# Encoder layer on one core: value products of a query-tile pair on aligned key blocks, with one 128-column product for both edge blocks

## The chip, the cores and the metric

The kernel runs on one core of a Trainium2 chip. The metric is the device time of one execution in microseconds (us). Three runs of the kernel before gave 2041.09, 2041.80 and 2042.51 us, median 2041.80.

## The reference

One encoder layer over 1024 tokens of width 1024: a half-step SwiGLU block, a hybrid mixer and a second half-step SwiGLU block, each followed by a layer norm. The change lies in the mixer's attention branch. It has twelve heads of width 128 in three groups of four, with windows and dilations (128,1), (512,4) and (2048,16):

```python
def dilated_window_attention(q, k, v, rel_bias_g, window, dilation):
    half = window // (2 * dilation)      # 64 in all three groups
    ...
    band = jnp.abs(off) <= half
    mask = band[None] & valid[:, None, :]
    logit_add = jnp.where(mask[None], bias[:, None], NEG_INF)
    s = einsum(q, k) * scale + logit_add
    mx = jnp.max(s, axis=-1, keepdims=True)
    p = jnp.exp(s - mx)
    den = jnp.sum(p, axis=-1)
    o = einsum(p, v) / den
```

A group with dilation d is d independent sequences of 1024/d tokens, and a query sees the keys at most 64 places away in its own sequence: group 0 is one sequence of 1024, group 1 four of 256, group 2 sixteen of 64. The weights p are exactly zero wherever the mask holds. The three groups' outputs are then joined by their softmax denominators, projected, gated and merged with a Fourier branch.

## The kernel before

All large matrix products (both SwiGLU blocks, the input projection, the output projection) are block products with seven multiplications for eight, in three float32r terms each. They are the jobs of the program: a fixed list for TensorE. Everything else is a node with a cost, a due time and the buffers it takes and gives back. A planner (`Flow`, L75 to L280) walks the job list at build time with a clock for each engine and writes out the order of each engine's instructions. Small TensorE work of the attention is a floating node (`F`): it is put between two jobs once its inputs are planned to be ready at least 0.8 us earlier. Loads (`Q`) go to SP's DMA queue, stores and a few loads to POOL's. At run time each engine and each queue works strictly in the written order and waits on semaphores.

The planner counts three pools: 8 PSUM banks, 46 pages of 128x1024 floats, and 11 halves of 128x512 floats (`NS2`, tag "s2"). A load that takes a half is put off while fewer than four others would remain free, unless its user is due within 5 us (L185). A load whose half is still being used by an earlier owner waits at the head of SP's queue, and whatever is behind it there waits too.

Attention of a head (`attention`, L1656) runs beside the projection jobs of the next head. It takes the head's query and key pages, its values (one page, `load_values`, L1623, three DMAs from DRAM in groups 0 and 1, rows of 128 floats) and its bias. The 1024 queries are cut into steps. A step is two query tiles of 128 in groups 0 and 1, four in group 2. Each step is one chain: `scores` on TensorE (L1685), `add_bias` and `top` on VectorE (L1699, L1709), `exps` on ScalarE (L1714), `turn` on TensorE (transposes of 128 columns, L1730), `turned` on ScalarE (PSUM to SBUF, L1739), `values` on TensorE (L1755, L1760), `keep` on ScalarE (L1773 to L1778).

Twenty of the forty steps are pairs with windows of 192 keys (`w == 192`, `split_`): the first and last tile of group 0's sequence, and both tiles of each of group 1's four sequences. They go like this before the change. The later tile comes first. The transposes give three blocks of 128 keys by 128 queries: the later tile's keys shifted by 64 with respect to the tiles, the earlier tile's keys shifted likewise, and a mixed block with 64 keys of each tile. `blank` (two VectorE memsets of 64x128, L1747, L1748) clears two quarters of the 256 columns that the mixed block is spread into, and `turned` copies the first two blocks (128x256) and then the mixed block's two halves (64x128 each, L1742, L1743). `values` makes one product of 256 columns of the mixed block's keys with both tiles (L1755) and two products of 128 columns (L1760). In group 0 the pair's order is turned round (`turned_round`, L1703), and `combine` reads group 1's statistics with the odd tiles first (L1996).

The planner also prepares pieces of the output projection's weights during this stage (`keep_halves`, L1932: 28 pieces, each one SP load, one ScalarE pass, one VectorE pass and two POOL stores, in three halves). `SPREAD` (L1887) chooses the jobs by which they are due.

Of the kernel before, what the change touches and what calls it, by code (L numbers as in the profile page):

```python
# [12 lines left out]
AF = mybir.ActivationFunctionType  # L13
# [3 lines left out]
P = 128  # L17
S0 = 1024
# [56 lines left out]
class Flow:  # L75
# [207 lines left out]
class Builder:  # L283
# [10 lines left out]
    def half(self, name, dt=F32):  # L294
        return self.sb.tile([P, 512], dt, name=name, tag="s2", bufs=NS2)
# [12 lines left out]
def kernel(  # L308
# [909 lines left out]
    VJ, v_stored, VW, vb, VT = {}, {}, {}, {}, {}  # L1218
# [48 lines left out]
    for i, (to, x0, x1) in enumerate((("t1", "b11", "b12"), ("t3", "b12", "b22"), ("t2", "t1", "b22"),  # L1267
# [6 lines left out]
        n = Q(J[("a", 1 + i), 4], 1.15, copy, [vtn[x0]] if x0 in vtn else [], lead=0.0)  # L1274
# [348 lines left out]
    def load_values(g, h):  # L1623

        c0 = (g * SLOTS + h) * P

        def rows(dst, row0, p_step, n, n_step):
            ap = [[p_step * QW, dst.shape[0]], [n_step * QW, n], [1, P]]
            nc.sync.dma_start(dst, bass.AP(tensor=v_d.tensor, offset=v_d.offset + row0 * QW + c0, ap=ap))
        t = page(f"v{g}{h}")  # L1630
        tv = as_k(t)
        vf = {}
        if g == 0:
            rows(tv[:, 0:7], 64, 1, 7, P)
            rows(tv[0:64, 7:8], S0 - 64, 1, 1, 1)
            rows(tv[64:128, 7:8], 0, 1, 1, 1)
            for i in range(7):
                vf[64 + P * i, P] = tv[:, i, :]
            vf["edge", 0] = tv[:, 7, :]
        elif g == 1:  # L1640
            rows(tv[:, 0:4], 4 * 64, 4, 4, 1)
            rows(tv[0:64, 4:8], 4 * 192, 4, 4, 1)
            rows(tv[64:128, 4:8], 0, 4, 4, 1)
            for i in range(4):
                vf[256 * i + 64, P] = tv[:, i, :]
                vf["edge", 256 * i] = tv[:, 4 + i, :]
# [9 lines left out]
    def attention(idx, g, h, qk, qk_nodes):  # L1656
        c = PC["q", idx]
        env = {}
        qv = Q(J[c, 4], 0.5, lambda: env.__setitem__("v", load_values(g, h)),
               [(n, 4.0) for m in range(8) for n in (v_stored[g, m] if g == 2 else [v_stored[g, m]])], 12.0, pages=1)  # L1660
        qb = Q(J[c, 4], 0.1, lambda: env.__setitem__("b", load_bias(g, h)),
               [(shear_n[g * SLOTS + h], 4.0)] + ([bias_done[idx - 2]] if idx >= 2 else []), 12.0)
        if g == 0:
            steps = [[(i, P * i - 64, 256) for i in (a, a + 1)] for a in (1, 3, 5)]
            steps.append([(7, S0 - 192, 192), (0, 0, 192)])
        elif g == 1:
            steps = [[(2 * r + 1, 256 * r + 64, 192), (2 * r, 256 * r, 192)] for r in range(4)]
        else:
            steps = [[(i, P * i, P) for i in range(a, a + 4)] for a in (0, 4)]
        col0 = 8 * g  # L1670
# [3 lines left out]
        def one(si, step):  # L1674
# [28 lines left out]
            turned_round = g == 0 and tiles == [0, 7]  # L1703

            def top():
                if h not in stats:
                    stats[h] = kb.small([P, 24, 2], "stat", bufs=2)
                cols = slice(7, None, -7) if turned_round else slice(s0, s0 + stepc * (n - 1) + 1, stepc)
                nc.vector.tensor_reduce(stats[h][:, cols, 0], p3(), AX.X, OP.max, negate=True)  # L1709

            def exps():
                for i in range(n):
                    k = 7 - 7 * i if turned_round else s0 + i * stepc
                    nc.scalar.activation(p3()[:, i, :], p3()[:, i, :], AF.Exp, bias=stats[h][:, k, 0:1], scale=1.0,  # L1714
                                         accum_out=stats[h][:, k, 1:2])
            (qa, ka, _), (qb_, kb_, _) = step[0], step[1]
            if w == 192:

                cuts = [0, 256, 128]
                where = [(qa, ka, P, 0, 0), (qb_, kb_ + 64, P, 0, 1), (qa, ka + P, 64, 0, 2), (qb_, kb_, 64, 64, 2)]  # L1720
# [11 lines left out]
            split_ = w == 192  # L1732

            def turned():
                if not split_:
                    st["t"] = half(f"pT{g}{h}{si}")
                t = st["t"]
                k = 2 * P if split_ else len(cuts) * P
                nc.scalar.activation(t[:, :k], st["tp"][:, :k], AF.Copy)  # L1739
                if split_:  # L1740

                    nc.scalar.activation(t[0:64, 3 * P:], st["tp"][0:64, k:k + P], AF.Copy)  # L1742
                    nc.scalar.activation(t[64:P, k:3 * P], st["tp"][64:P, k:k + P], AF.Copy)  # L1743

            def blank():
                st["t"] = half(f"pT{g}{h}{si}")
                nc.vector.memset(st["t"][0:64, 2 * P:3 * P], 0.0)  # L1747
                nc.vector.memset(st["t"][64:P, 3 * P:], 0.0)  # L1748

            def values():  # L1750
                st["o"] = bk = bank(f"pv{g}{h}{si}")
                seen = set()
                pt = st.pop("t")
                if split_:
                    nc.tensor.matmul(bk[:, :2 * P], env["v"]["edge", kb_], pt[:, 2 * P:], start=True, stop=False,  # L1755
                                     skip_group_check=True)
                for qt, kc, rows, r0, sl in where[:2] if split_ else where:
                    at = tiles.index(qt) * P
                    last = split_ or sum(x[0] == qt for x in where) == 1 + (qt in seen)
                    nc.tensor.matmul(bk[:, at:at + P], env["v"][kc, rows], pt[:, sl * P:(sl + 1) * P],  # L1760
                                     start=not split_ and qt not in seen, stop=last, skip_group_check=True)
                    seen.add(qt)

            def keep():
                if "pv" not in env:
# [214 lines left out]
    def combine(h):  # L1980
# [18 lines left out]

# [559 lines left out]
```

## Time and profile before

| what | value |
|---|---|
| median of three runs | 2041.80 us (2041.09 to 2042.51) |
| the profiled execution's own time | 2041.54 us |
| its span, first to last instruction | 2039.8 us |
| TensorE busy | 2028.7 us |
| VectorE, ScalarE, POOL busy | 1372.8, 907.5, 283.2 us |
| granted TensorE clock | 0.999 |

The span is 1.74 us shorter than the execution's own time. In the trace a float32 product is two matmul records (two passes), a float32r product or a transpose is one; records of neighbouring matmuls overlap, so what a matmul costs is read from the start of one to the start of the next. PE is TensorE's matmuls, PEld its weight loads, SPq and POOLq are DMA issues of the two queues, and a number in square brackets behind a row is the idle time of the engine before it, with what ended it.

### The profile page before, as it was taken

What the parts mean: (1) busy time and instruction counts of PE and PEld (TensorE: products, weight loads), DVE (VectorE), ACT (ScalarE), POOL (GpSimd) and SP (SyncE); (2) the same over time, 40 slices, a digit from 0 to 9 for tenths busy, and PEclk for the clock granted to TensorE, in tenths of its full rate; (3) what the DMA queues carried; (4) which work ended last, traced back from release to release, by engine and by line L of the source; (5) the groups of instructions that cost most, each with busy time, mean ns of one, the idle gap of its engine ahead of it and who ended that gap; (6) DMA issues with size and microseconds to landing.
All of it is one profiled execution on the core that took longest, in us unless ns stands there. A gap on an engine that the chain in (4) does not pass through costs nothing.

```text
span 2039.8 us, 26286 instructions
## 1 busy us (share of the span) xinstructions
PE 2028.7 (99%) x9531; PEld 1700.2 (83%) x9531; DVE 1372.8 (67%) x1988; ACT 907.5 (44%) x1440; POOL 283.2 (14%) x486
## 2 busy tenths in 40 slices
PE   9999999999999999999999999999999999999998
PEld 7888888888888898888888888888888888888886
DVE  7765665576676768665656666887876665575565
ACT  6433333454454224655556444336533333355432
POOL 0133211111001122222122110000011111110000
PEclk9999999999999999999999999999999999999999
DMA  5789998899953366655345669784157887668752
GB/s 206 234 269 284 292 299 260 248 338 369 339 186 130 115 242 212 217 182 153 118 134 169 228 224 348 279 328 170 68 195 232 267 250 215 177 214 288 236 186 94
DMA packets 179251, 458.52 MB, mean 225 GB/s; under 512 B 21362, under 2 KB 55490, under 8 KB 178576
## 3 DMA queue, kind: packets, MB, share of 16 engines
q1 hardware_dynamic: 130864, 299.42, 42.5%
q0 software_dynamic: 48256, 157.41, 25.8%
q8 instruction: 75, 1.23, 0.2%
q14 instruction: 56, 0.46, 0.1%
HBM read 341.69 MB, written 185.29 MB: 258 GB/s over the span
## 4 chain that ended last, share of the span: by engine, by line
PE 98%; DMA 1%; ACT 1%; DVE 0%; issue 0%; SPq 0%; DVEq 0%
PE Ab L496 14%; PE Aa L496 14%; PE Aq L496 8%; PE Db L496 6%; PE Da L496 6%; PE As L496 5%; PE Dq L496 3%; PE Zb L865 3%; PE Xa L865 3%; PE Xb L865 3%; PE Za L865 3%; PE Ds L496 2%; PE wA L2384 2%; PE Va L865 1%; PE Vb L865 1%; PE Yb L865 1%
## 5 line engine op out<-in xcount | busy, mean ns | idle before, releaser
L1714 ACT ACTIVATE p<-p,stat 128x192 f32<-128x192 f32 (+2 forms) x96 | 42.2, 441 | 24.0 <-DVE stat L1709 22.4
L338 POOL DMA_DIRECT2D n_spill<-y x16 | 9.4, 586 | 300.8 <-DVE y L1062 244.4
L338 POOL DMA_DIRECT2D hsba<-t2b x21 | 11.6, 550 | 265.6 <-DVE t2b L731 265.6
L338 POOL DMA_DIRECT2D hsaa<-t2a x21 | 12.4, 589 | 244.8 <-DVE t2a L731 240.0
L1504 DVE SCALAR_TENSOR_TENSOR oq<-Dq,b_cols,t2q 128x512 f32<-128x512 f32 x12 | 11.8, 985 | 50.3 <-PE Dq L496 50.3
L634 ACT ACTIVATE t2b<-Ab 128x512 f32<-128x512 f32 x21 | 12.6, 598 | 63.5 <-PE Ab L496 63.5
L727 DVE TENSOR_TENSOR t2b<-Db,t2b 128x512 f32<-128x512 f32 x21 | 14.5, 691 | 39.1 <-PE Db L496 39.1
L1699 DVE SCALAR_TENSOR_TENSOR p<-sc,bias 128x512 f32<-128x512 f32 (+1 forms) x40 | 24.8, 621 | 20.6 <-PE sc L1685 18.7
L727 DVE TENSOR_TENSOR t2a<-Da,t2a 128x512 f32<-128x512 f32 x21 | 14.5, 690 | 35.3 <-PE Da L496 35.3
L634 ACT ACTIVATE t2a<-Aa 128x512 f32<-128x512 f32 x21 | 12.5, 596 | 55.7 <-PE Aa L496 55.7
L1760 PEld LDWEIGHTS pv<-pT,v 128*128 128x128 f32 x240 | 32.6, 191 | 3.4 <-ACT pT L1739 1.0
L1685 PE MATMUL sc<-oq,oq 128*128 128x192 f32 (+2 forms) x192 | 34.8, 322 | 0.0
L1760 PE MATMUL pv<-pT,v 128*128 128x128 f32 x240 | 33.0, 275 | 0.6 <-ACT pT L1739 0.6
L1685 PEld LDWEIGHTS sc<-oq,oq 128*128 128x128 f32 x192 | 29.4, 190 | 1.7
L719 DVE TENSOR_TENSOR t3b<-Db,t3b 128x512 f32<-128x512 f32 x21 | 14.5, 691 | 22.1 <-PE Db L496 20.0
L496 PE MATMUL Da<-Xs40h,usa 128*128 128x512 f32 x84 | 29.3, 389 | 0.0
L496 PE MATMUL Da<-Xs41h,usa 128*128 128x512 f32 x84 | 29.3, 389 | 0.0
L496 PE MATMUL Db<-Zs40h,usb 128*128 128x512 f32 x84 | 29.3, 389 | 0.0
L496 PE MATMUL Db<-Zs41h,usb 128*128 128x512 f32 x84 | 29.3, 389 | 0.0
L719 DVE TENSOR_TENSOR t3a<-Da,t3a 128x512 f32<-128x512 f32 x21 | 14.5, 690 | 21.6 <-PE Da L496 18.3
L1709 DVE TENSOR_REDUCE stat<-p 128x2 f32<-128x384 f32 (+2 forms) x40 | 24.3, 619 | 1.0
L634 ACT ACTIVATE t3a<-Aa 128x512 f32<-128x512 f32 x21 | 12.5, 596 | 26.9 <-PE Aa L496 26.8
(7647 smaller groups left out, 7428.9 us busy)
## 6 DMA issues: line engine op xcount, KB each, us to landing
qa<-hsas SPq DMA_DIRECT2D x43, 256.0 KB, 6.8
qa<-tdat SPq DMA_DIRECT2D x43, 256.0 KB, 5.4
qb<-hsbs SPq DMA_DIRECT2D x43, 256.0 KB, 4.3
ga<-in_ffn_gu_dram SPq DMA_DIRECT2D x21, 512.0 KB, 8.9
ua<-in_ffn_gu_dram SPq DMA_DIRECT2D x21, 512.0 KB, 10.0
gb<-in_ffn_gu_dram SPq DMA_DIRECT2D x21, 512.0 KB, 4.6
ub<-in_ffn_gu_dram SPq DMA_DIRECT2D x21, 512.0 KB, 5.8
qb<-tdbt SPq DMA_DIRECT2D x33, 256.0 KB, 5.0
```

The lines of the kernel that those rows point to most:

```text
L338: nc.gpsimd.dma_start(*a, **kw)
L496: nc.tensor.matmul(out, pick(w, a)[:, k * P:(k + 1) * P], self.cols(xn, b, k), start=first and k == 0 and ti == 0, stop=last and k == kt - ...
L634: nc.scalar.activation(H[c, t], B[c, "B"], AF.Copy)
L719: nc.vector.tensor_sub(H[c, "t3"], B[c, "D"], H[c, "t3"])
L727: nc.vector.tensor_sub(H[c, "t2"], B.pop((c, "D")), H[c, "t2"])
L865: nc.tensor.matmul(bank_, a, b, start=first and ti == 0, stop=last and ti == len(todo) - 1, skip_group_check=True)
L1685: nc.tensor.matmul(sv[:, i, :], qk[0][:, qt * P:(qt + 1) * P], qk[1][:, k0:k0 + w], start=True, stop=True, skip_group_check=True)
L1699: stt(p3(), sv, scale, bv, op0=OP.mult, op1=OP.add)
L1709: nc.vector.tensor_reduce(stats[h][:, cols, 0], p3(), AX.X, OP.max, negate=True)
L1714: nc.scalar.activation(p3()[:, i, :], p3()[:, i, :], AF.Exp, bias=stats[h][:, k, 0:1], scale=1.0, accum_out=stats[h][:, k, 1:2])
L1760: nc.tensor.matmul(bk[:, at:at + P], env["v"][kc, rows], pt[:, sl * P:(sl + 1) * P], start=not split_ and qt not in seen, stop=last, skip_ ...
L2384: nc.tensor.matmul(B["w", bk, m], X4.cols(xn, a, k)[:, m * P:(m + 1) * P], pick(w, b), start=new and k == 0 and ti == 0, stop=k == 3 and t ...
```

## The change

In a split pair the earlier tile now comes first. Its first 128 columns of weights are its own 128 keys, and columns 64 to 192 of the later tile are the later tile's own 128 keys: key blocks that are aligned with the query tiles. The middle block has 64 keys of the later tile for the earlier tile's queries (in its upper 64 rows) and 64 keys of the earlier tile for the later tile's queries (in its lower 64 rows). By the mask only the second 64 queries of the earlier tile see the former, and only the first 64 queries of the later tile see the latter. Two quarters of the block are therefore zero by the exponential itself. With its two column halves swapped in the copy, the block is one operand of 128 columns for the output columns 64 to 192.

So the memsets go, three ScalarE copies become two, and the product of 256 columns becomes one of 128 which comes last and accumulates over both tiles' columns. The values are loaded in aligned blocks of 128 keys and, for the edges, into a half (`te`): five DMAs in place of three for a head of group 0 (640 KB in place of 512), four in place of three for one of group 1 (768 KB in place of 512). The half is taken with the load and given back after the head's last value product. The view of the bias goes through its 64-column step downwards, the statistics' columns lose their turned order, and the planner's costs of the changed nodes and `SPREAD` (14 to 10, so all 28 pieces of output weights are due four jobs earlier) are set anew.

```diff
+        te = half(f"ve{g}{h}").rearrange("p (k n) -> p k n", k=4) if g < 2 else None
         if g == 0:
             rows(tv[:, 0:7], 64, 1, 7, P)
-            rows(tv[0:64, 7:8], S0 - 64, 1, 1, 1)
-            rows(tv[64:128, 7:8], 0, 1, 1, 1)
+            rows(tv[:, 7:8], 0, 1, 1, 1)
+            rows(te[:, 0:1], S0 - P, 1, 1, 1)
+            rows(te[0:64, 1:2], P, 1, 1, 1)
+            rows(te[64:128, 1:2], S0 - 192, 1, 1, 1)
...
         elif g == 1:
-            rows(tv[:, 0:4], 4 * 64, 4, 4, 1)
-            rows(tv[0:64, 4:8], 4 * 192, 4, 4, 1)
-            rows(tv[64:128, 4:8], 0, 4, 4, 1)
+            for i in range(2):
+                rows(tv[:, 4 * i:4 * i + 4], 4 * P * i, 4, 4, 1)
+                rows(te[64 * i:64 * i + 64], 4 * (P - 64 * i), 4, 4, 1)
...
         qv = Q(J[c, 4], 0.5, lambda: env.__setitem__("v", load_values(g, h)),
-               [...], 12.0, pages=1)
+               [...], 12.0, pages=1, halves=int(g < 2))
...
-            steps.append([(7, S0 - 192, 192), (0, 0, 192)])
+            steps.append([(0, 0, 192), (7, S0 - 192, 192)])
         elif g == 1:
-            steps = [[(2 * r + 1, 256 * r + 64, 192), (2 * r, 256 * r, 192)] for r in range(4)]
+            steps = [[(2 * r, 256 * r, 192), (2 * r + 1, 256 * r + 64, 192)] for r in range(4)]
...
-                    bv = bass.AP(tensor=bias.tensor, offset=bias.offset, ap=[list(bias.ap[0]), [64, 2], [1, 192]])
+                    bv = bass.AP(tensor=bias.tensor, offset=bias.offset + 64, ap=[list(bias.ap[0]), [-64, 2], [1, 192]])
...
                 nc.scalar.activation(t[:, :k], st["tp"][:, :k], AF.Copy)
                 if split_:
-                    nc.scalar.activation(t[0:64, 3 * P:], st["tp"][0:64, k:k + P], AF.Copy)
-                    nc.scalar.activation(t[64:P, k:3 * P], st["tp"][64:P, k:k + P], AF.Copy)
-
-            def blank():
-                st["t"] = half(f"pT{g}{h}{si}")
-                nc.vector.memset(st["t"][0:64, 2 * P:3 * P], 0.0)
-                nc.vector.memset(st["t"][64:P, 3 * P:], 0.0)
+                    to, at = (x[:, k:k + P].rearrange("p (s q) -> p s q", s=2) for x in (t, st["tp"]))
+                    nc.scalar.activation(to, at[:, ::-1, :], AF.Copy)
...
-                if split_:
-                    nc.tensor.matmul(bk[:, :2 * P], env["v"]["edge", kb_], pt[:, 2 * P:], start=True, stop=False,
-                                     skip_group_check=True)
-                for qt, kc, rows, r0, sl in where[:2] if split_ else where:
+                for qt, kc, rows, r0, sl in where:
...
+                if split_:
+                    nc.tensor.matmul(bk[:, 64:192], env["v"]["edge", ka], pt[:, 2 * P:3 * P], start=False, stop=True,
+                                     skip_group_check=True)
...
-            nb = [V(0.35, blank, [n2], slack=8.0, halves=1)] if split_ else []
-            n4 = S(0.95 if split_ else 0.54, turned, [f2] + nb, frees=1, halves=0 if split_ else 1, slack=8.0)
-            f3 = F(0.88 if split_ else 0.22 * len(where), values, [n4], 1, hgives=1, gives=1 if end else 0)
+            n4 = S(0.6 if split_ else 0.54, turned, [f2], frees=1, halves=1, slack=8.0)
+            f3 = F(0.22 * (len(where) + int(split_)), values, [n4], 1, hgives=1 + int(end and g < 2), gives=1 if end else 0)
...
-    SPREAD = lambda k: 2 * k + 14
+    SPREAD = lambda k: 2 * k + 10
...
-                gather(t[32 * j:32 * j + 32, 1], 8 + 4 * (1 - j), 0, [[4 * 48, 32], [48, 4], [1, 8]])
+                gather(t[32 * j:32 * j + 32, 1], 8 + 4 * j, 0, [[4 * 48, 32], [48, 4], [1, 8]])
```

More of the change, by code (lines that the diff above doesn't have):

```diff
@@ L1634, in load_values @@
             rows(tv[:, 0:7], 64, 1, 7, P)
-            rows(tv[0:64, 7:8], S0 - 64, 1, 1, 1)
-            rows(tv[64:128, 7:8], 0, 1, 1, 1)
+            rows(tv[:, 7:8], 0, 1, 1, 1)
+            rows(te[:, 0:1], S0 - P, 1, 1, 1)
+            rows(te[0:64, 1:2], P, 1, 1, 1)
+            rows(te[64:128, 1:2], S0 - 192, 1, 1, 1)
             for i in range(7):
                 vf[64 + P * i, P] = tv[:, i, :]
-            vf["edge", 0] = tv[:, 7, :]
+            vf[0, P] = tv[:, 7, :]
+            vf[S0 - P, P] = te[:, 0, :]
+            vf["edge", 0] = te[:, 1, :]
         elif g == 1:
-            rows(tv[:, 0:4], 4 * 64, 4, 4, 1)
-            rows(tv[0:64, 4:8], 4 * 192, 4, 4, 1)
-            rows(tv[64:128, 4:8], 0, 4, 4, 1)
+            for i in range(2):
+                rows(tv[:, 4 * i:4 * i + 4], 4 * P * i, 4, 4, 1)
+                rows(te[64 * i:64 * i + 64], 4 * (P - 64 * i), 4, 4, 1)
+            for i in range(8):
+                vf[256 * (i % 4) + P * (i // 4), P] = tv[:, i, :]
             for i in range(4):
-                vf[256 * i + 64, P] = tv[:, i, :]
-                vf["edge", 256 * i] = tv[:, 4 + i, :]
+                vf["edge", 256 * i] = te[:, i, :]
         else:
@@ L1659, in attention @@
         qv = Q(J[c, 4], 0.5, lambda: env.__setitem__("v", load_values(g, h)),
-               [(n, 4.0) for m in range(8) for n in (v_stored[g, m] if g == 2 else [v_stored[g, m]])], 12.0, pages=1)
+               [(n, 4.0) for m in range(8) for n in (v_stored[g, m] if g == 2 else [v_stored[g, m]])], 12.0, pages=1,
+               halves=int(g < 2))
         qb = Q(J[c, 4], 0.1, lambda: env.__setitem__("b", load_bias(g, h)),
@@ L1701, in one @@
             s0, stepc = (col0 + tiles[0] // 2, 4) if g == 1 else (col0 + tiles[0], tiles[1] - tiles[0])
-            turned_round = g == 0 and tiles == [0, 7]
             def top():
@@ L1719, in one @@
                 cuts = [0, 256, 128]
-                where = [(qa, ka, P, 0, 0), (qb_, kb_ + 64, P, 0, 1), (qa, ka + P, 64, 0, 2), (qb_, kb_, 64, 64, 2)]
+                where = [(qa, ka, P, 0, 0), (qb_, kb_ + 64, P, 0, 1)]
             else:
@@ L1734, in turned @@
             def turned():
-                if not split_:
-                    st["t"] = half(f"pT{g}{h}{si}")
-                t = st["t"]
+                st["t"] = t = half(f"pT{g}{h}{si}")
                 k = 2 * P if split_ else len(cuts) * P
@@ L1753, in values @@
                 pt = st.pop("t")
+                for qt, kc, rows, r0, sl in where:
+                    at = tiles.index(qt) * P
+                    last = not split_ and sum(x[0] == qt for x in where) == 1 + (qt in seen)
+                    nc.tensor.matmul(bk[:, at:at + P], env["v"][kc, rows], pt[:, sl * P:(sl + 1) * P],
+                                     start=not seen if split_ else qt not in seen, stop=last, skip_group_check=True)
+                    seen.add(qt)
                 if split_:
-                    nc.tensor.matmul(bk[:, :2 * P], env["v"]["edge", kb_], pt[:, 2 * P:], start=True, stop=False,
+                    nc.tensor.matmul(bk[:, 64:192], env["v"]["edge", ka], pt[:, 2 * P:3 * P], start=False, stop=True,
                                      skip_group_check=True)
-                for qt, kc, rows, r0, sl in where[:2] if split_ else where:
[L1758 to L1762, printed above, removed]
             def keep():
```

5 lines of the change are left out of this document (2 added, 3 removed).

## The prediction

> **What bounds the kernel now.** I read the page's busy times and chain first, then who waits for whom on TensorE, then busy time by stage (in each row the stretch, its length, and PE, PEld, DVE, ACT, POOL, granted clock, DMA share, GB/s).
>
> ```profile
> span 2039.8 us, 26286 instructions
> ...
> PE 2028.7 (99%) x9531; PEld 1700.2 (83%) x9531; DVE 1372.8 (67%) x1988; ACT 907.5 (44%) x1440; POOL 283.2 (14%) x486
> ...
> PE 98%; DMA 1%; ACT 1%; DVE 0%; issue 0%; SPq 0%; DVEq 0%
> ```
>
> ```profile
> PE warm L2463 <- DVE eps L334: 1.4, 1, 1.4
> PE Aa L496 <- ACT Xa110h L386: 0.8, 1, 0.8
> PE pv L1760 <- ACT pT L1739: 0.6, 1, 0.6
> PE Aa L496 <- DVE Xa110l L392: 0.2, 1, 0.2
> ```
>
> ```profile
> 784.73:1122.43 337.70, 337.14 (x1734) 288.43 (x1733) 213.81 (x354) 197.28 (x460) 71.37 (x126) 1.00 0.56 173
> 1122.43:1270.00 147.57, 147.57 (x685) 123.38 (x685) 98.06 (x131) 69.36 (x98) 19.67 (x36) 1.00 0.73 262
> 1270.00:1410.00 140.00, 140.00 (x723) 119.37 (x722) 111.80 (x216) 54.24 (x97) 2.17 (x4) 1.00 0.71 267
> 1410.00:2029.00 619.00, 619.00 (x2749) 512.97 (x2748) 410.42 (x536) 251.23 (x340) 59.42 (x101) 1.00 0.64 205
> ```
>
> TensorE makes 98% of the chain, at full granted clock. It idles only in the first microseconds, in the tail after its last matmul, and once in between: 0.56 us in the attention stage (784.73 to 1122.43), before a value product. So a microsecond of product removed there is a microsecond off the time, as long as the work that follows is ready that much earlier; and what VectorE (214 of 338 us) or ScalarE (197) is spared is worth nothing by itself.
>
> **The change part by part.** First the products. The rows give start, duration and count of records. Two split pairs stand next to each other here; a step of four 128-column products follows:
>
> ```profile
> 851.31 0.59 PE L1755 MATMUL pv<-pT,v 128*128 128x256 f32 x2
> 851.74 0.61 PE L1760 MATMUL pv<-pT,v 128*128 128x128 f32 x4
> 852.18 0.60 PE L1755 MATMUL pv<-pT,v 128*128 128x256 f32 x2
> 852.62 0.61 PE L1760 MATMUL pv<-pT,v 128*128 128x128 f32 x4
> ```
>
> ```profile
> 820.48 1.05 PE L1760 MATMUL pv<-pT,v 128*128 128x128 f32 x8
> 821.37 0.60 PE L1730 MATMUL pt<-ident,p 128*128 128x128 f32 x4
> ```
>
> Start to start, the 256-column product takes 0.43 to 0.44 us (851.31 to 851.74), two products of 128 columns take 0.44 (851.74 to 852.18), so 0.22 each; the four take 0.89, again 0.22. A split pair's values cost 0.87 us before and 3 x 0.22 = 0.66 to 0.67 after: 0.20 to 0.21 less. There are 20 such pairs (four heads, one in group 0 and four in group 1); the by-form group counts 40 records of two passes each:
>
> ```profile
> L1755 PE MATMUL pv<-pT,v 128*128 128x256 f32 x40 | 11.9, 378 | 0.0
> ```
>
> That is 20 x 0.21 = 4.2 us (4.0 to 4.4 by the rounding of the rows). The new product comes last and accumulates over the second half of one tile and the first half of the other. No row shows an accumulation across two outputs; bounded by 0.22 (a 128-column product) and 0.44 (the one it replaces), I take 0.22, because today's products accumulate over columns just written at that price. The lower bound cannot be undercut: the columns are streamed. Weight loads stay at three per pair.
>
> The Trainium skill (TensorE: Matmul & The Clock Gate, Back-to-back issue gap) gives 134 cycles for an isolated matmul of 128 columns and 262 for 256, but says that in a real stream of load and matmul the weight load counts too, and that 128 columns then take about 81 ns in place of 56. With four units of the page's gap for a product of float32, an estimate, the isolated figures give 0.22 and 0.44 us, as the rows above do; by the sustained figure a 128-column product would be 0.32 us, and twenty would gain about 2 us in place of 4.2 (this is rival 3). The trace does not agree with the sustained figure.
>
> Next ScalarE and VectorE, one split pair:
>
> ```profile
> 831.54 0.38 ACT L1739 ACTIVATE pT<-pt 128x256 f32<-128x256 f32 x1
> 831.82 0.26 ACT L1742 ACTIVATE pT<-pt 64x128 f32<-64x128 f32 x1
> 832.09 0.27 ACT L1743 ACTIVATE pT<-pt 64x128 f32<-64x128 f32 x1
> ```
>
> ```profile
> 829.07 0.17 DVE L1747 MEMSET pT<- 64x128 f32 x1
> 829.30 0.17 DVE L1748 MEMSET pT<- 64x128 f32 x1
> ```
>
> VectorE loses 40 memsets of 0.17 us, each 0.23 from start to start: 9 us. ScalarE trades two copies of 0.26 and 0.27 for one of 128x128 with its halves swapped, between 0.26 (64x128) and 0.38 (128x256); I take 0.27, nearest to the same column count, so 20 x 0.26 = 5 us less. Both engines have over 120 us free in the stage, so I count zero. The gain cannot be more than the 0.56 us of TensorE's one wait there; if the swapped copy cost the full 0.38, the chain of a pair would still be 0.15 us shorter than now. The bias view that steps backwards and the statistics' new columns keep their instruction count and shapes: between zero and, if the backward step slowed the 384-element pass, the 0.1 us between its 0.55 and the 0.69 of a 512-element one, 20 times, beside TensorE's jobs: zero.
>
> Now the loads. The rows of SP's queue come first; TensorE's first use of the first head's values is the row at 820.48 above, and of the second head's the one at 851.31:
>
> ```profile
> 785.83 3.05 SPq L1629 DMA_DIRECT2D v<-v_spill  x3
> ...
> 807.76 2.15 SPq L1629 DMA_DIRECT2D v<-v_spill  x3
> ```
>
> ```profile
> DMA to landing us min/median/max: 3.2/6.7/10.7
> ```
>
> Four heads get two DMAs more and four one more, 12 issues at about 0.7 us (2.15/3) on SP: 9 us of queue in 338, and 1.5 MB at 173 GB/s, 9 us of transfer at a DMA share of 0.56. Values are issued 35 and 44 us ahead of use and land within 10.7, so even a doubled issue and landing (3 and 11 us) stays hidden: zero. What stands behind them in SP's queue is the next pair's weights, treated under the rivals; POOL's queue gets nothing.
>
> The half `te` is held from the load to the head's last value product: 785.83 to 834.5 and 807.76 to 861.2, about 50 us. Eight heads in 338 us hold 8 x 50 / 338 = 1.2 of the 11 halves on average, two at times. Against this the split step takes its output half only at `turned`, not at `blank` (829.07 to 831.54, 2.5 us, so 20 x 2.5 / 338 = 0.15 halves). The pool gets tighter by about one. This delays nodes that want a half, first the 28 weight pieces, whose users are products of a later stage. `SPREAD` makes these due four jobs earlier, about 4 x 2.75 = 11 us (a job is a row such as the one below) plus the floats between. All of a piece moves: one SP load, one ScalarE and one VectorE pass, two POOL stores. They cross loads of values and pair weights on SP and the bias and spill stores on POOL; TensorE reads none of them in this stage, so zero.
>
> ```profile
> 960.52 2.74 PE Aq L496 x12
> ```
>
> Last, the planner: with other costs it writes another order from here to the end. The later stages have TensorE busy in 147.57 of 147.57 us, 140.00 of 140.00 and 619.00 of 619.00; I count zero, and bound it by a gain of 0.56 (the one wait) and a loss of 2.2, four waits of that size.
>
> The sum: the profiled execution's 2041.54 - 4.2 = 2037.3 us. Its own time is 0.26 below the median of the runs, 2041.8, which is what the new runs will be set against: 2041.8 - 4.2 = 2037.6; with a little of the one wait gone, 2037.5. The 0.2% that a measurement of this kernel can tell from no change is 4.1 us, so the forecast lies on that edge.
>
> **The rivals.**
>
> (1) The saved columns come back as waits. The place is the end of the attention, where the last head's exponentials meet the first gate's sigmoids on ScalarE:
>
> ```profile
> 1105.78 1.28 ACT L1496 ACT_TABLE_LOAD   x1
> 1107.07 0.69 ACT L1496 ACTIVATE os<-As,b_cols 128x512 f32<-128x512 f32 x1
> 1107.78 1.28 ACT L1714 ACT_TABLE_LOAD   x1
> 1109.07 0.40 ACT L1714 ACTIVATE p<-p,stat 128x128 f32<-128x128 f32 x1
> ...
> 1111.11 0.57 ACT L1739 ACTIVATE pT<-pt 128x512 f32<-128x512 f32 x1
> ```
>
> ```profile
> 1111.74 0.49 PE L1760 MATMUL pv<-pT,v 128*128 128x128 f32 x2 [0.56 <-ACT pT L1739]
> ```
>
> Two table loads of 1.28 us lie ahead of the copy that TensorE's only wait is for. The planner does not know them. If the new order puts one more sigmoid between the last steps, two more loads come: 2.6 us on that chain, 2037.5 + 2.6 = 2040.1. If it puts the sigmoid after the last step, the wait goes: 2037.0. For it speaks that this chain has no cover left. Against: it is one place, and the first gate is due when it was. The Trainium skill (ScalarE: Activation LUTs, What ACT_TABLE_LOAD costs) puts a switch at 1283 ns and a further 1380 ns of drain; by it two more switches would be 5.3 us and the time 2042.8, an estimate. The load agrees with the rows; the drain they do not show, since the exponential starts 1.29 us after its load.
>
> (2) Slower: the tighter halves block SP's queue. It happens today that a piece waits at the head of the queue for a half which is still being stored (the row gives total, times and longest wait):
>
> ```profile
> SPq L1941 <- DMA wot_d<-wot10l: 12.2, 1, 12.2
> ```
>
> ```profile
> 880.14 0.33 SPq L570 DMA_DIRECT2D uq<-in_in_pairs_dram  x1
> 880.53 2.30 SPq L1629 DMA_DIRECT2D v<-v_spill  x3
> 883.00 12.16 SPq L1941 DMA_DIRECT2D wot40r<-wtt  x2
> 905.39 0.33 SPq L570 DMA_DIRECT2D gq<-in_in_pairs_dram  x1
> ```
>
> ```profile
> 915.44 0.48 PE L496 MATMUL Aq<-Ys20h,t12q7h 128*128 128x512 f32 x1
> ```
>
> Now a values load can wait there too, with pair weights behind it. The weights issued at 880.14 feed the product at 915.44, 35 us later. Landing, taken at the 10.7 us of the slowest values load, and the sums and splits in between leave some 20 us, an estimate: a block must exceed that before TensorE stops. Two blocks like the longest one here, back to back (24.3 us), stop it for 4.3 and eat the gain: 2041.8. Three (36.5) give 2037.5 + 16.5 = 2054. Against: no stop shows today with blocks of 12, the pieces now finish earlier, and the planner puts off values loads while the pool is short.
>
> (3) The change does not do what it says: the 128-column edge product is held by its weight loads (records of 0.19 us, two passes, 0.38 us) and not by its columns. It would then save 0.43 - 0.38 = 0.05, in all 1 us: 2040.8. Against: the same loads precede today's 128-column products, which follow each other at 0.22.
>
> ```profile
> L1755 PEld LDWEIGHTS pv<-pT,v 128*128 128x128 f32 x40 | 7.1, 189 | 1.2
> ```
>
> **How the numbers follow.** The forecast, 2036.9 to 2038.2 for itself: 0.58, of which 0.35 lies beyond the 0.2% edge (2037.7). The wait gone or more (2036.2 to 2036.9): 0.07, faster. Rival 1's loss, or other small waits from a new order (2038.2 to 2042): 0.19, within 0.2%. Rival 3: 0.03, within. Rival 2, from 2042 up: 0.13, about 0.11 of it slower by more than 0.2% (over 2045.9). So faster 0.42, same 0.47, slower 0.11. The range 2036.2 to 2042.0 takes in both bounds of the unknowns and leaves out rival 2.
>
> **What would show it.** No 256-column record in the value products, three starts 0.22 apart in a split pair, the copies down to two per pair at 0.38 and about 0.27, no memsets, 4.2 us fewer between the first and the last projection job of the attention stage, and TensorE's waits no longer than one 0.6. The prediction is wrong if a wait on ScalarE or a DMA of over 1 us appears among TensorE's waits, if the values' first product waits for its load, or if SP's waits at the values' line pass 20 us.

## The result and the profile after

The changed kernel takes 2036.47 us (median; 2036.13 to 2037.19) beside 2041.64 for the kernel before, a ratio of 0.9975 with a 95% interval of 0.9965 to 0.9984: 5.2 us, 0.25% faster. The profiled execution took 2036.13 us, its span 2034.3.

The page of the changed kernel, busy time and chain:

```profile
span 2034.3 us, 26254 instructions
...
PE 2025.1 (100%) x9531; PEld 1697.1 (83%) x9531; DVE 1366.1 (67%) x1948; ACT 900.2 (44%) x1418; POOL 283.0 (14%) x486
...
PE 99%; DMA 1%; DVE 0%; ACT 0%; issue 0%; SPq 0%; DVEq 0%
```

All waits of TensorE in it:

```profile
PE warm L2460 <- DVE eps L334: 1.4, 1, 1.4
PE Aa L496 <- DVE Xa110l L392: 0.2, 1, 0.2
```

The wait before a value product is gone; what is left lies in the first microseconds. To see where the time went, the two traces are cut at the same TensorE instructions: the first product with the weights of the first query pair, the first product of the Fourier channels (L2069 before, L2066 after), the first product of the second SwiGLU block, and the last of all. Columns as before: the stretch, its length, then PE and the others. The kernel before:

```profile
785.63:1260.99 475.36, 474.80 (x2342) 402.39 (x2340) 306.36 (x468) 263.07 (x549) 89.69 (x160) 1.00 0.60 196
1260.99:1410.63 149.64, 149.64 (x798) 128.56 (x796) 117.04 (x233) 57.81 (x105) 3.53 (x7) 1.00 0.73 274
1410.63:2031.41 620.78, 620.78 (x2756) 514.44 (x2755) 409.79 (x536) 251.23 (x340) 59.42 (x101) 1.00 0.64 205
```

The changed kernel:

```profile
785.09:1255.86 470.77, 470.77 (x2342) 399.31 (x2341) 299.09 (x426) 254.10 (x525) 87.56 (x156) 1.00 0.61 199
1255.86:1405.58 149.72, 149.72 (x798) 128.57 (x797) 117.05 (x233) 57.86 (x105) 3.53 (x7) 1.00 0.73 272
1405.58:2026.44 620.86, 620.86 (x2756) 514.43 (x2755) 409.86 (x536) 251.60 (x340) 59.34 (x101) 1.00 0.63 205
```

The first stretch, called the stage below, holds the whole attention and is 475.36 - 470.77 = 4.59 us shorter; the two later ones are 0.16 longer together. Of the 5.5 us between the spans the rest is 0.54 before 785 and 0.53 behind the start of the last product. The front moves by that much between profiled executions: in the ten other kernels below that have eleven halves the stage begins anywhere between 785.33 and 786.17. The tail is 7.80 to 8.06 us in the kernels made from the changed one and 8.01 to 8.39 in those made from the one before, some 0.3 apart on average; what makes that difference I did not find. So I compare stages in the traces and medians in the times.

A split pair's values in the changed kernel, followed by the transposes of another step:

```profile
846.83 0.60 PE L1755 MATMUL pv<-pT,v 128*128 128x128 f32 x4
847.27 0.39 PE L1759 MATMUL pv<-pT,ve 128*128 128x128 f32 x2
847.50 0.49 PE L1735 MATMUL pt<-ident,p 128*128 128x128 f32 x3
```

Two products in 0.44 and the edge product in 0.23: 0.67 us, where it was 0.87 to 0.88. The copy with swapped halves, by form:

```profile
L1746 ACT ACTIVATE pT<-pt 128x128 f32<-128x128 f32 x20 | 5.5, 274 | 0.0
```

0.274 us, as the 64x128 copies were.

### The profile page after: what moved, and what is told of

Its sections match the earlier page's. It is cut to its first block, busy times and chain, and to the rows that moved or that the text cites. A ratio compares the mean times of both kernels' runs of the same rounds, so it can differ in the third digit from the quotient of the medians.

```text
span 2034.3 us, 26254 instructions
## 1 busy us (share of the span) xinstructions
PE 2025.1 (100%) x9531; PEld 1697.1 (83%) x9531; DVE 1366.1 (67%) x1948; ACT 900.2 (44%) x1418; POOL 283.0 (14%) x486
## 4 chain that ended last, share of the span: by engine, by line
PE 99%; DMA 1%; DVE 0%; ACT 0%; issue 0%; SPq 0%; DVEq 0%
PE Ab L496 14%; PE Aa L496 14%; PE Aq L496 8%; PE Db L496 6%; PE Da L496 6%; PE As L496 5%; PE Dq L496 3%; PE Zb L865 3%; PE Xb L865 3%; PE Za L865 3%; PE Xa L865 3%; PE Ds L496 2%; PE wA L2381 2%; PE sc L1692 2%; PE Va L865 1%; PE Vb L865 1%
## 5 line engine op out<-in xcount | busy, mean ns | idle before, releaser
L634 ACT ACTIVATE t2b<-Ab 128x512 f32<-128x512 f32 x21 | 12.6, 600 | 63.8 <-PE Ab L496 63.8
L634 ACT ACTIVATE t2a<-Aa 128x512 f32<-128x512 f32 x21 | 12.6, 598 | 56.3 <-PE Aa L496 56.3
L634 ACT ACTIVATE t3a<-Aa 128x512 f32<-128x512 f32 x21 | 12.6, 598 | 26.9 <-PE Aa L496 24.7
## 6 DMA issues: line engine op xcount, KB each, us to landing
ua<-in_ffn_gu_dram SPq DMA_DIRECT2D x21, 512.0 KB, 10.2
```

What stands on the lines that cost most here:

```text
L634: nc.scalar.activation(H[c, t], B[c, "B"], AF.Copy)
```

## The experiments

After the result my theory was that the columns pay 4.2 us and that the 0.56 us wait goes with the new order of the work. The rivals were that the 128-column product is held by its weight loads, that the gain is the order's or the lighter engines', and that the halves or SP's queue take something back.

**The columns alone, in the old order.** The edge product loses half its columns and nothing else moves.

```diff
-                    nc.tensor.matmul(bk[:, :2 * P], env["v"]["edge", kb_], pt[:, 2 * P:], start=True, stop=False,
+                    nc.tensor.matmul(bk[:, :P], env["v"]["edge", kb_], pt[:, 2 * P:3 * P], start=True, stop=False,
```

> The kernel before in its own order, with one edit: the edge product of a split pair takes the first 128 of its 256 columns (the edge keys of one tile of the pair are left out, so the output is not the reference's). This is the column term alone. Theory (columns pay, and the one wait of 0.56 us before a value product stays because the order of the work stays): 20 x 0.21 = 4.2 us less than before, 2041.6 - 4.2 = 2037.4, some 0.9 above the changed kernel, and the wait of TensorE on the copy of pT is still in the trace. Rival (the weight loads hold a 128-column product): 1 us less, 2040.6. Rival (the gain is the new order's or the lighter VectorE's and ScalarE's): no change, 2041.6.

2037.04 us beside 2041.49: 4.45 less. Its stage, and its wait of TensorE:

```profile
785.33:1256.59 471.26, 470.70 (x2342) 399.27 (x2340) 306.23 (x468) 263.14 (x549) 89.69 (x160) 1.00 0.61 198
```

```profile
PE pv L1760 <- ACT pT L1739: 0.6, 1, 0.6
```

The stage is 475.36 - 471.26 = 4.10 us shorter, 0.205 per product, and the wait is still there. The column theory holds and both rivals fall. The kernel leaves out the edge keys of one tile of each pair, and keeps the order and the other engines' work. Between it and the changed one stand 0.57 us in the medians and 0.49 in the stage.

**The columns put back, in the new order.** One more product of 128 columns per pair.

```diff
                     nc.tensor.matmul(bk[:, 64:192], env["v"]["edge", ka], pt[:, 2 * P:3 * P], start=False, stop=True,
                                      skip_group_check=True)
+                    nc.tensor.matmul(bk[:, 256:384], env["v"]["edge", ka], pt[:, 2 * P:3 * P], start=True, stop=True,
+                                     skip_group_check=True)
```

> The changed kernel in its own order, with one more 128-column product per split pair, of the same operands into an unused part of the PSUM bank (its result is not read). Theory: the column term is given back, 20 x 0.22 = 4.4 us, 2036.5 + 4.4 = 2040.9, and no wait of TensorE in the attention stage; what is then left against the kernel before, 0.7 us, is the new order's. Rival (the gain is the order's): 2036.5 to 2037.

2040.63 us, 4.2 more than the changed kernel, and a stage of 474.87, again 4.10 more:

```profile
785.40:1260.27 474.87, 474.87 (x2382) 403.99 (x2381) 299.02 (x426) 254.04 (x525) 87.58 (x156) 1.00 0.62 197
```

Both directions give the same price. What is left against the kernel before is 0.49 us of stage.

**More weight loads, no more columns.**

```diff
-                    nc.tensor.matmul(bk[:, 64:192], env["v"]["edge", ka], pt[:, 2 * P:3 * P], start=False, stop=True,
-                                     skip_group_check=True)
+                    for c in (0, 64):
+                        nc.tensor.matmul(bk[:, 64 + c:128 + c], env["v"]["edge", ka], pt[:, 2 * P + c:2 * P + c + 64],
+                                         start=False, stop=c == 64, skip_group_check=True)
```

> The changed kernel in its own order, with the edge product cut into two of 64 columns, each with its own weight load: 20 weight loads more, no column more. Theory (columns alone count): two products of 0.11 us, 2036.5 to 2037. Rival (weight loads bind below some width): if a pass cannot follow the last one faster than the 0.11 us at which 128-column passes follow each other, the two cost 0.44 in place of 0.22, 20 x 0.22 = 4.4 us more, 2040.9; if a pass takes a whole weight load's 0.19 us, 0.76 in place of 0.22, 2047.3. It tells how near to its weight loads the new 128-column product already is.

2040.39 us, 3.9 more than the changed kernel: here the rival is right. The pair's rows and the stage:

```profile
847.47 0.60 PE L1755 MATMUL pv<-pT,v 128*128 128x128 f32 x4
847.91 0.56 PE L1760 MATMUL pv<-pT,ve 128*128 128x64 f32 x4
848.30 0.50 PE L1735 MATMUL pt<-ident,p 128*128 128x128 f32 x3
```

```profile
785.51:1260.32 474.81, 474.81 (x2381) 403.43 (x2380) 298.93 (x426) 254.17 (x525) 87.55 (x156) 1.00 0.61 196
```

By the stage, 4.04 / 20 = 0.20 us for each product more: two products of 64 columns cost nearly what two of 128 cost, and half the columns save nothing. Is it the weight load that holds such a pass, or a least time of any pass? Rows of the changed kernel's next stretch tell them apart. Each first row is four passes, with the size of their weights (128*128, 128*4) and of their output:

```profile
1265.76 0.51 PE L2137 MATMUL fse<-fev,chan 128*128 128x2 f32 x4
1266.12 0.37 PE L2108 MATMUL fp<-posp0h,fold 128*128 128x256 f32 x1
```

```profile
1269.16 0.24 PE L2173 MATMUL fsem<-chan,fev 128*4 128x1 f32 x4
1269.34 0.28 PE L2108 MATMUL fpm<-posp0h,fmid 128*4 128x256 f32 x1
```

Passes of 2 columns with weights of 128 columns take 0.09 us each, start to start (0.36 / 4); with weights of 4 columns a pass takes under 0.05 (0.18 / 4). So, as far as these rows go, it is the weight load of 128 columns that holds a pass at about 0.1 us, however few columns follow it. The 128-column product, at two passes of 0.11, stands just at that floor, and whether its columns or its weight loads hold it these rows cannot tell. As long as each pass has its own weight load of 128 columns, the change took the last factor of two that columns can give here. The Trainium skill (TensorE: Matmul & The Clock Gate, LDWEIGHTS) puts a weight load of 128 columns at 128/1.2 = 107 ns; by that, an estimate, twenty more products of two passes cost 20 x 2 x 0.107 = 4.3 us. The measured 4.04 is 6% below that.

**The spared work of VectorE and ScalarE put back.**

```diff
                     nc.scalar.activation(to, at[:, ::-1, :], AF.Copy)
+                    nc.scalar.activation(t[:, 3 * P:], st["tp"][:, k:k + P], AF.Copy)
...
                 nc.vector.tensor_reduce(stats[h][:, cols, 0], p3(), AX.X, OP.max, negate=True)
+                if w == 192:
+                    nc.vector.memset(st["p"][0:64, 3 * P:], 0.0)
+                    nc.vector.memset(st["p"][64:P, 3 * P:], 0.0)
```

> The changed kernel in its own order, with the removed VectorE and ScalarE work put back as work on unused columns: two memsets of 64x128 after each split pair's maximum, and one more 128x128 copy from PSUM after its two copies (40 memsets, 20 copies; the results are not read). Theory (both engines have room, so what they were spared is worth nothing): 2036.5, within 0.5. Rival (part of the gain is theirs, through shorter chains): up to 1 us more, with waits of TensorE on ScalarE in the attention stage.

2036.39 us, and a stage of 470.77, the changed kernel's to the hundredth:

```profile
785.43:1256.20 470.77, 470.77 (x2342) 399.31 (x2340) 305.86 (x466) 257.37 (x545) 87.58 (x156) 1.00 0.62 198
```

VectorE is busy 7 us longer, ScalarE 3, and nothing follows. The busy time that these engines were spared is worth nothing. (The memsets stand behind the maximum here; that the copies wait for them, as in the kernel before, is not put back.)

**The table loads taken out of the kernel before.** The order of every engine stays; only one function of ScalarE and its table loads change.

```diff
-        nodes = pair_out(PC["s", c], [COL_G + c * P, COL_G + D + c * P], gs, plain_view, AF.Sigmoid)
+        nodes = pair_out(PC["s", c], [COL_G + c * P, COL_G + D + c * P], gs, plain_view, AF.Sigmoid if c else AF.Exp)
```

> The kernel before in its own order, with the first gate pair's sigmoid replaced by an exponential (so that pair's gates are wrong): the same ScalarE work, but the three table loads at 1105.78, 1107.78 and 1111.70 us go, of which two lie ahead of the copy that TensorE's only wait is for. Theory (the wait that the change also removed is made by these loads): no wait of TensorE in the attention stage, 0.56 us less than before, 2041.1. Rival (the wait is the chain's length or the buffers'): 2041.6, and the wait stays in the trace.

2040.86 us beside 2041.71, 0.85 less. Its waits of TensorE are all in the first microseconds, and the stage is 475.36 - 474.54 = 0.82 us shorter:

```profile
PE warm L2463 <- DVE eps L334: 1.4, 1, 1.4
PE Aa L496 <- DVE Xa111l L392: 0.2, 1, 0.2
PE Aa L496 <- ACT Xa111h L386: 0.2, 1, 0.2
```

```profile
786.17:1260.71 474.54, 474.54 (x2341) 402.49 (x2340) 306.15 (x468) 260.55 (x547) 89.66 (x160) 1.00 0.60 197
```

So these loads make the wait. (One of the three comes back at 1126.05, before the next sigmoid, where TensorE does not wait.) They cost 0.26 us more than the wait's row shows, because the row counts only from the end of the record before. Start to start, the value product comes 0.95 us behind the last product of the job in the kernel before (1110.79 to 1111.74) and 0.23 in this one, and its first pass then takes 0.21 us in place of 0.11. In the changed kernel the last exponential comes before the first sigmoid, and one load stands where there were three:

```profile
1101.93 0.19 ACT L1719 ACTIVATION_READ_ACCUMULATOR p<-p,stat 128x1 f32 x1
1102.14 1.28 ACT L1496 ACT_TABLE_LOAD   x1
1103.43 0.69 ACT L1496 ACTIVATE os<-As,b_cols 128x512 f32<-128x512 f32 x1
...
1110.43 0.68 ACT L1515 ACTIVATE os<-t3s,b_cols 128x512 f32<-128x512 f32 x1
```

**Which edit moved the exponentials?** Three kernels change the written order alone: the changed kernel with the old `SPREAD`, the kernel before with the new one, and the changed kernel with the planner's old costs.

```diff
-    SPREAD = lambda k: 2 * k + 10
+    SPREAD = lambda k: 2 * k + 14
```

> The changed kernel with the due times of the 28 pieces of output weights put back (SPREAD 2k + 14): the one edit of the change that is a choice. Theory (this work touches no product of the stage and only the order moves): 2036.5, within 1. Rival (the change needs it, since the half held by the edge values leaves too few): waits of TensorE in the attention stage or SP blocked at the pieces, 2038 or more.

```diff
-    SPREAD = lambda k: 2 * k + 14
+    SPREAD = lambda k: 2 * k + 10
```

> The kernel before with SPREAD 2k + 10 alone. Theory: 2041.6, within 1. Rival (the earlier due times themselves bring part of the gain, for instance the wait and the two table loads at the end of the attention): 2041.0 or less, with four table loads in place of six around the end of the attention.

```diff
-            n4 = S(0.6 if split_ else 0.54, turned, [f2], frees=1, halves=1, slack=8.0)
-            f3 = F(0.22 * (len(where) + int(split_)), values, [n4], 1, hgives=1 + int(end and g < 2), gives=1 if end else 0)
+            n4 = S(0.95 if split_ else 0.54, turned, [f2], frees=1, halves=1, slack=8.0)
+            f3 = F(0.88 if split_ else 0.22 * len(where), values, [n4], 1, hgives=1 + int(end and g < 2), gives=1 if end else 0)
```

> The changed kernel with the planner's old costs for the copies and the value products of a split pair (0.95 and 0.88 in place of 0.60 and 0.66): the same work in another order. Theory: the columns' gain stays, 2036.5 to 2038, depending on whether the last exponentials come before the first sigmoids; if six table loads stand around the end of the attention, TensorE's wait is back and the time is some 0.6 above the changed kernel's. Rival (the order makes much of the gain): over 2039.

| kernel | us | stage, us | table loads at the end of the attention |
|---|---|---|---|
| before | 2041.64 | 475.36 | three (1105.78, 1107.78, 1111.70) |
| before, SPREAD 10 | 2040.71 | 474.43 | one (1106.83) |
| changed | 2036.47 | 470.77 | one (1102.14) |
| changed, SPREAD 14 | 2036.45 | 470.57 | one (1102.27) |
| changed, old costs | 2036.25 | 470.45 | one (1102.35) |

`SPREAD` alone moves the sigmoid in the kernel before and brings it 0.9 us: here the rival was right. In the changed kernel the sigmoid comes late with either value and with either set of costs. Neither of these two edits is needed for it. The old order had the sigmoid between the last two steps, and each of these changes of order leaves it; I take that for an accident of the order. Among the changed kernel's orders, all with one load, stages differ by 0.3 us. What makes that is not shown, but it goes with how often TensorE passes from a small product of the attention to a job: counted in the traces, 65 times in the changed kernel's stage, 63 with `SPREAD` 14 and 60 with the old costs (61 in the kernel before).

**The loads.** The values loaded twice, and three times (the last loop then runs over `again + again`), each round behind the one before in SP's queue.

```diff
-            nc.sync.dma_start(dst, bass.AP(tensor=v_d.tensor, offset=v_d.offset + row0 * QW + c0, ap=ap))
+            again.append((dst, bass.AP(tensor=v_d.tensor, offset=v_d.offset + row0 * QW + c0, ap=ap)))
+            nc.sync.dma_start(*again[-1])
+        again = []
...
+        if g < 2:
+            for dst, src in again:
+                nc.sync.dma_start(dst, src)
```

> The changed kernel in its own order, with every values load of groups 0 and 1 issued a second time right behind the first ones, into the same tiles, so that the second must wait for the first: 36 more DMAs, 5.5 MB more, and SP's queue blocked about 6 us longer for each of eight heads. Theory (values are due 35 us and more after their issue, and pair weights behind them about 20): 2036.5, within 0.5. Rival (SP's queue is near its limit with the tighter halves): waits of TensorE on a load or on the sums and splits behind it, 2038 or more.

> The changed kernel with the values of groups 0 and 1 loaded three times, each round waiting for the one before. Loading them twice cost 1.0 us over the runs (2037.49), while the trace showed its attention stage as long as the changed kernel's. Theory A (an SP block of this length is still hidden, and the 1.0 us is a transfer that sometimes lands late): 2037.5 to 2038.5, growing with the number of loads, with a wait of TensorE on a load or a sum behind one in the trace. Theory B (the queue's block is what costs): over 2040. Theory C (the 1.0 us is between programs and not the loads): 2037.5, no more than with two.

Twice: 2037.49 us, 1.0 more than the changed kernel and more than the theory allowed, though in its trace the stage is 470.76 and TensorE waits nowhere in it; the profiled execution was its fastest (2036.81). Three times: 2041.11, 4.6 more, and here the trace shows it. TensorE's waits in the stage, ScalarE's wait that leads to the first of them, and SP's rows ahead of that:

```profile
818.80 0.93 PE L1740 MATMUL pt<-ident,p 128*128 128x128 f32 x4 [0.81 <-ACT p L1724]
889.82 0.50 PE L496 MATMUL Aq<-Ys20h,t12q6h 128*128 128x512 f32 x1 [0.77 <-ACT Aq L629]
913.84 1.16 PE L1760 MATMUL pv<-pT,v 128*128 128x128 f32 x8 [0.98 <-ACT pT L1747]
```

```profile
814.16 1.06 ACT L358 ACTIVATE gq4h<-gq 128x1024 fp32r<-128x1024 f32 x1 [4.42 <-DMA gq<-in_in_pairs_dram]
```

```profile
806.72 2.15 SPq L1662 DMA_DIRECT2D ve<-v_spill  x3
808.98 0.54 SPq L570 DMA_DIRECT2D gq<-in_in_pairs_dram  x1
```

In the changed kernel the same weights are issued at 800.06:

```profile
800.06 0.34 SPq L570 DMA_DIRECT2D gq<-in_in_pairs_dram  x1
```

They are issued 8.9 us later here, 7.8 from the stage's start, which lies 1.1 later in this trace. They land 5.2 us behind their issue (at most 4.6 in the changed kernel), so it is mostly the issue that is late. This makes ScalarE stand 4.4 us before the weights' split. The product with these weights starts only at 833.1, but behind the split in ScalarE's order stand the first head's exponentials, and TensorE's transposes wait 0.8 us for these. The three waits are 2.6 us by their rows and 3.6 from start to start, of the 3.8 by which the stage is longer (474.56 - 470.77). The queue's block is what costs (theory B), though through an engine in between; the chain is followed for the first wait only. What the 1.0 us of the second load is, its trace does not show. ScalarE already stands 0.49 us there for the same weights, so that it is the same chain in slower executions is likely but stays open.

**The halves.** One half fewer, in both kernels.

```diff
-NS2 = 11
+NS2 = 10
```

> The changed kernel with ten halves of 128x512 in place of eleven, so one less on top of the one that the edge values hold. Theory (the halves are not at their limit; the planner finds an order without waits): 2036.5 to 2038. Rival (the tighter halves are what the change pays, and one more brings waits behind SP's queue): 2040 or more, with SP's waits at the values' line or the pieces' line over 20 us or waits of TensorE in the attention stage.

> The kernel before with ten halves in place of eleven: the tightening that the edge values bring, on average, without the change. Theory: 2041.6, within 1. Rival (halves bind): 2043 or more, and more than what ten halves cost the changed kernel would then show that the change eases the halves instead of tightening them.

The kernel before goes from 2041.71 to 2045.75 (4.0 more; its runs spread from 2044.10 to 2050.25), the changed one from 2036.47 to 2050.46 (14.0 more). Both theories missed: ten halves are too few for either kernel, and the changed one loses more. The loss is not where I had looked for it. SP's waits in the stage stay under 21 us, at the values' line under 18 and at the pieces' line under 13. TensorE's longest wait stands behind the attention, near the end of the stage, for a weight load that is issued late:

```profile
PE pB L496 <- DMA wpt0h<-wpt_d: 7.6, 1, 7.6
PE wB L1249 <- DVE wtt3l L363: 1.5, 1, 1.5
PE warm L2460 <- DVE eps L334: 1.4, 1, 1.4
PE Ds L496 <- DVE t3s L1510: 1.2, 1, 1.2
```

That load goes out at 1250.1 here and at 1236.9 in the changed kernel, 10.2 us later from the stage's start, and lands after 12.6 us in place of 9.5. By the stretches the loss is 3.0 us before the stage, 7.1 in it and 4.8 in the next one. But in this order the stage holds 19 passes fewer (2323 in place of 2342), some 4.3 us of work that now lies behind the cut, so the stage loses about 11.4 and the next stretch 0.5. The waits of 7.6 and 1.2 us and the slower clock after the first of them (2.3, last section) make most of that. Of the 3.0 before the stage, 1.5 are the wait at L1249, ahead of the attention, and 1.0 more waiting in the first microseconds. The kernel before with ten halves waits at L1249 too, for 1.8 us. So part of the loss has nothing to do with the edge values. Why the planner's order for ten halves brings that load late, and whether the half of the edge values is the reason, is not shown.

## Why the prediction was right, point by point

The forecast was 2037.5, the range 2036.2 to 2042.0; measured 2036.47. The direction and the main term are right, the gain is larger by 0.9 us; 0.16 more lies in the base, 2041.64 where the forecast started from 2041.80. The time lies only 0.27 us inside the range, in its part from 2036.2 to 2036.9, to which I had given a chance of 0.07. What carries it there is not the change itself but the order that came with it, which is luck as far as the forecast goes.

- The products, 4.2 us (4.0 to 4.4): 4.10 by the stage, in both directions, 4.45 and 4.2 by the medians. The step holds, and so does the choice of 0.22 for the accumulation across two outputs (0.205 by the difference of stages).
- The one wait, of which I let "a little" go (0.1 us): this is the term that was mis-sized. It went in full, and it was larger than the 0.56 us that I read from its row and used as a bound: the table loads are worth 0.82 us in the kernel before. Rival 1 named the place and gave 2037.0 for this outcome, a time that lies in the forecast's own part (2036.9 to 2038.2), while I had put "the wait gone" below 2036.9; the two do not fit. The order was disturbed throughout, and of seven orders on record, two of them with ten halves, only the old one has the sigmoid between the last steps. A wait that hangs on such a coincidence is more likely to go than to stay when everything is ordered anew.
- 4.10 + 0.49 = 4.59 us is the stage's gain. Columns and table loads by themselves make 4.10 + 0.82 = 4.92, so the new order takes 0.33 back; that fits the 0.3 by which orders differ. Of the 0.6 us that the medians show beyond the stage, some 0.3 may be the tail's; the cause of that stays open.
- VectorE's 9 us and ScalarE's 5 us at zero: right as far as tested, the work put back costs nothing. The swapped copy at 0.27: 0.274.
- The new order of the later stages at zero, bounded by 2.2: the two stretches are 0.16 us longer.
- The loads at zero: right for the change as made. The reason given for it was half wrong. I estimated that SP could be blocked 20 us before TensorE stops, from the issue of the weights to their product. In the experiment a delay of 8 was enough. I had not asked what is queued behind the weights' first reader on ScalarE.
- `SPREAD` at zero: right in the changed kernel (0.02 us). In the kernel before it is worth 0.9.
- Rival 2, the tighter halves: did not happen at eleven. One fewer costs 14 us against 4 before, so the halves are near their limit, but not by its mechanism: no wait at the values' or the pieces' line reached 20 us (17.2 and 12.4 at most), and TensorE's long wait is for a weight load behind the attention.
- Rival 3, weight loads hold the product: its price was wrong, since a pass with its load takes 0.11 us and not the 0.19 of the load's record, which overlaps its neighbours. But the weight loads do set a floor, and between 64 columns, which cost as much, and 256, which cost twice as much, 128 is the width at which it begins to bind.

## What to carry to other kernels

Where one engine works without a gap, count its instructions by start-to-start times and multiply: the price of a removed product was right to a tenth of a microsecond. The few waits that remain are not part of that price and depend on the order; look at what makes each (here two table loads that the planner does not know) and ask whether a new order would keep it. A wait is best read from start to start as well, since its row showed 0.56 of 0.82 us here. A free-looking buffer is worth testing by taking one more away: with one half fewer the kernel before lost 4 us and the changed one 14, so the next change that takes a half cannot count it as free.

## What the runs showed of the hardware

A float32 product with its own weight load of 128 columns got no cheaper when its 128 columns became 64: each product of 64 columns added cost 0.20 us, the same as one of 128. Passes of 2 columns still took 0.09 us behind weights of 128 columns, and under 0.05 behind weights of 4. And TensorE's clock fell in its long wait in the changed kernel with ten halves. The columns are the stretch, its length, PE, granted clock, DMA share and GB/s:

```profile
1254.80:1262.80 8.00, 0.42 (x2) 0.86 1.03 419
1262.80:1267.40 4.60, 4.57 (x14) 0.50 1.03 411
1267.40:1270.00 2.60, 2.60 (x25) 1.00 1.02 402
1270.00:1280.00 10.00, 10.00 (x80) 1.00 0.53 211
```

The granted clock is half for 4.6 us after a wait of 7.6 us and full again after that, so this wait costs some 2.3 us beside itself (4.6 x 0.5). The Trainium skill (TensorE: Matmul & The Clock Gate, Why this matters for your kernels) says that idle gaps of more than about 3 us throttle the clock; the rows agree for 7.6 us, and no run here tests the 3. The rows also show the DMA engines full (1.03) while the weights are awaited.
